# Down stage of an encoder layer: seven products on shared PSUM banks, with kept operands and a reordered end

## The chip, the cores and the metric

The kernel runs on one core of a Trainium2 chip. The metric is the device time of one execution in microseconds (us), lower is better; a kernel's time is the median of its runs.

## The reference, cut to what matters

One encoder layer (a token mixer, then a gated feed-forward block with a convolution of width 3) runs on 256 + 1024 = 1280 tokens of 1024 channels, all in fp32. The change lies in the last matrix product and in what follows it:

```python
D_FF = ((8 * D_MODEL // 3 + 127) // 128) * 128        # 2816
def conv_ffn(h, w_up, w_conv, b_conv, w_down):
    ...
    gate, val = jnp.split(up, 2, axis=-1)
    return (jax.nn.silu(gate) * val) @ w_down
...
        y = conv_ffn(h, w_up[l], w_conv[l], b_conv[l], w_down[l])
        x = x + gate2 * rmsnorm(y, g_post_ffn[l])
```

So y = G · W, G of 1280 x 2816 and W (`w_down`) of 2816 x 1024, then a root-mean-square norm of each row of y, a gain per column and an addition to x.

## The kernel before, in words

**Products.** TensorE takes every fp32 matrix product as three products of operands that are each split into a high and a low part (`split`, L89: ScalarE rounds the high part to fp32r, VectorE subtracts it from the source to get the low part). `mmk` (L1150) issues the three 128 x 128 by 128 x 512 matmuls high·high, high·low and low·high into one PSUM bank.

**Strassen.** The Down stage halves each of the three dimensions and uses Strassen's seven products M1 to M7 in place of eight block products. G is kept transposed in DRAM (`g_d`, one tensor per 128 of the 2816 inner rows), and its blocks are A00, A01, A10, A11 (first index: the half of the tokens, 640 each; second: even or odd 128-row slice of the inner dimension). B00 to B11 are the blocks of W (first index: the same even or odd slice; second: the half of the 1024 output columns). Each product has 11 steps k over 128 inner rows and 5 tiles j of 128 tokens, so 11 · 5 · 3 = 165 matmuls. The table `prods` (L1311) gives the order M3, M5, M1, M7, M4, M2, M6, the operands of each (a block, or a sum or difference of two blocks) and where its result goes: output block (half of the tokens, half of the columns) and how (`set`, `neg`, `add`, or subtract).

**Steps.** `ops_of(i, k)` (L1322) loads the blocks of a step with DMAs on SyncE's queue, makes the sum or difference on VectorE (`saM` of 640 columns for A, `sbM` of 512 for B, L1330) and splits both into `aoM` and `boM`. Rings limit how far this runs ahead: 4 tiles for A loads, 4 raw tiles for B loads (`raw_d`), 2 for each sum, 4 for `aoM`, 5 for `boM`. The diagonal blocks A00 and A11 stay on chip from their first load (`ares`, L1273), and so does B11 for the first 7 steps (`bres`, L1274). All other blocks are loaded again for each product that uses them.

**Banks.** Each product takes 5 of the 8 PSUM banks in rotation (`bank`, L1145), one per tile j; 3 of them were not used by the product before. After two starting steps, which are run together for the tiles 0, 1, 2 and then for 3, 4, TensorE goes step by step over all five tiles. The last 2 steps (the last 4 of M6) are run tile by tile, and after each tile `evac` (L1372) brings the bank to the output rows `y` in SBUF: ScalarE copies (`set`, `neg`), VectorE adds or subtracts.

**End of a block.** When the last product that goes into an output block is in, `finish` (L1339) takes the sum of squares on ScalarE (`junk`) and multiplies by the gain on VectorE (`yg`, L1345). When both column halves of a tile are finished, `emit` (L1351) makes the row factor `rf` on GpSimd (L1359, L1360). For the tiles of the first half of the tokens, ScalarE scales the rows and GpSimd starts an adding DMA to the output, spread over the steps of the next product (`later`). For the second half, whose tiles end in M6, x was put into the output earlier and is loaded again into `xo` (three buffers, L1365); VectorE multiplies by `rf` and adds (L1368, two halves of 512 columns), and SyncE's queue stores each half (L1370).

**Order.** TensorE's order is the program's. The instructions of ScalarE, VectorE, GpSimd and SyncE's queue are put in order within each engine by a planner from its own estimate of times and the order of the program as priority; on the chip each queue then runs strictly in that order, so an instruction that waits holds up what stands behind it.

Of the kernel before, what the change touches and what calls it, by code (L numbers as in the profile page):

```python
# [8 lines left out]
F32 = mybir.dt.float32  # L9
# [3 lines left out]
AF = mybir.ActivationFunctionType  # L13
ALU = mybir.AluOpType
# [20 lines left out]
def encoder_kernel(ctx: ExitStack, tc: tile.TileContext, x_prompt, x_sample, c_prompt, c_sample,  # L35
# [3 lines left out]
    nc = tc.nc  # L39
# [13 lines left out]
    def out_rows(t):  # L53
        return out_p[0, P * t:P * t + P, :] if t < 2 else out_s[0, P * (t - 2):P * (t - 1), :]
# [34 lines left out]
    def split(w, raw, eng=None):  # L89
        nc.scalar.activation(w[:, 0, :], raw, AF.Copy)  # L90
        (eng or nc.gpsimd).tensor_tensor(out=w[:, 1, :], in0=raw, in1=w[:, 0, :].bitcast(F32), op=ALU.subtract)  # L91
# [327 lines left out]
    for ev in CFG["ord"].split():  # L419
# [6 lines left out]
        else:  # L426
            f = affine_h1 if ev[0] in "AB" else low_h1
# [388 lines left out]
    for g in range(4 * NT):  # L816
        gi, t = g // NT, g % NT
# [71 lines left out]
    with tc.high_priority():  # L889
# [14 lines left out]
                                   op0=ALU.add, op1=ALU.mult)  # L904
# [175 lines left out]
    for f in range(F0):  # L1080
        ps = fp.tile([P, 2, 256], F32, tag="f", name=f"upP_{f}")
        ws = []
        for half in range(2):
            for kh in range(2):
                with tc.issue_after(mloads[6].ins if f == 0 else xloads[NT - 1].ins) if f < 2 else ExitStack():
                    raw = load_up(f, half, kh, f"raw_p{f}_{half}{kh}")
                w = fslot(f"wp{f}_{half}{kh}")
# [57 lines left out]
    def bank(name):  # L1145
        i = banks["i"] % 8
        banks["i"] += 1
        return gpa.tile([P, 512], F32, tag="g", name=name) if i in (3, 4) else fp.tile([P, 512], F32, tag="f", name=name)

    def mmk(ps, ao, w, j, k):  # L1150
        cs_ = slice(P * j, P * j + P)
        for q, (ai, wi) in enumerate(((0, 0), (0, 1), (1, 0))):
            nc.tensor.matmul(ps, ao[ai][:, cs_], w[wi], start=(k == 0 and q == 0), stop=(k == NK - 1 and q == 2))  # L1153
# [129 lines left out]
    for k in range(NK - 1, NE - 1, -1):  # L1283
        new_ar(0, k)
        if k < 7:
            new_br(k)
    loaded = set()

    def load_a(r, c, k):
        if r == c:  # L1290
            if (r, k) not in loaded:
                loaded.add((r, k))
                nc.sync.dma_start(ares[(r, k)], g_d[2 * k + c][r])
            return ares[(r, k)]
        t = new_as(f"A{r}{c}_{k}")
        nc.sync.dma_start(t, g_d[2 * k + c][r])
        return t

    def load_b(c, n, k):
        if c and n and ("b", k) in loaded:  # L1300
            return bres[k]
        f = 2 * k + c
        if c and n and k < 7:
            raw = bres[k]
            loaded.add(("b", k))
        else:
            raw = raw_tile(f"raw_d{c}{n}_{k}")
        nc.sync.dma_start(raw, w_down[P * f:P * f + P, 512 * n:512 * n + 512])
# [9 lines left out]
    y, ygs = {}, {}  # L1318
    ssq = {t: dn.tile([P, 2], F32, name=f"fssq{t}") for t in range(NT)}
    done = set()  # L1320

    def ops_of(i, k):  # L1322
        name, a, b, _ = prods[i]
        src = []
        for what, terms, load, n, tag in ((0, a, load_a, 640, "sa"), (1, b, load_b, 512, "sb")):
            t0 = load(*terms[0], k)
            if len(terms) > 1:
                t1 = load(*terms[1], k)
                s = new_sum(tag, n, f"{tag}{name}_{k}")
                nc.vector.tensor_tensor(out=s, in0=t0, in1=t1, op=ALU.add if terms[2] > 0 else ALU.subtract)  # L1330
                t0 = s
            src.append(t0)
        ao = new_ao(f"ao{name}_{k}")
        split(ao, src[0], nc.vector)
        wo_ = new_bo(f"bo{name}_{k}")
        split(wo_, src[1], nc.vector)
        return [[t[:, h, :] for h in range(2)] for t in (ao, wo_)]

    def finish(t, n):  # L1339
        junk = dn.tile([P, 512], BF16, tag="junk", name=f"junk{t}_{n}", bufs=1)  # L1340
        cs_ = slice(512 * n, 512 * n + 512)
        nc.scalar.activation(junk, y[t][:, cs_], AF.Square, scale=1.0 / 32, accum_out=ssq[t][:, n:n + 1])  # L1342
        yg = y[t][:, cs_] if (t, 1 - n) not in done else dn.tile([P, 512], F32, tag="yg" if t in half_tiles[1] else "yh", name=f"yg{t}", bufs=2 if t in half_tiles[1] else 5)
        ygs[(t, n)] = yg
        nc.vector.tensor_tensor(out=yg, in0=y[t][:, cs_], in1=Gbc2[:, 0 if t < 2 else 1, cs_], op=ALU.mult)  # L1345
# [3 lines left out]
    later = []  # L1349

    def emit(t, n):  # L1351
        def scaled():
            for n in range(2):
                cs_ = slice(512 * n, 512 * n + 512)
                nc.scalar.activation(y[t][:, cs_], ygs[(t, n)], AF.Copy, scale=r)
                nc.gpsimd.dma_start(out_rows(t)[:, cs_], y[t][:, cs_], accum_op=ALU.add)

        r = dn.tile([P, 1], F32, tag="rf", name=f"rf{t}", bufs=6)
        nc.gpsimd.tensor_tensor(out=r, in0=ssq[t][:, 0:1], in1=ssq[t][:, 1:2], op=ALU.add)  # L1359
        nc.gpsimd.tensor_tensor(out=r, in0=r, in1=mhalf, op=ALU.pow)  # L1360
# [4 lines left out]
        nc.sync.dma_start(xo, out_rows(t))  # L1365
        for n in range(2):
            cs_ = slice(512 * n, 512 * n + 512)
            nc.vector.scalar_tensor_tensor(out=xo[:, cs_], in0=ygs[(t, n)], scalar=r, in1=xo[:, cs_],  # L1368
                                           op0=ALU.mult, op1=ALU.add)
            nc.sync.dma_start(out_rows(t)[:, cs_], xo[:, cs_])  # L1370

    def evac(i, j, ps):  # L1372
        for r, n, how in prods[i][3]:
            t = half_tiles[r][j]
            if t not in y:
                y[t] = dn.tile([P, D], F32, name=f"y{t}")
            d = y[t][:, 512 * n:512 * n + 512]
            if how == "set":
                nc.scalar.activation(d, ps, AF.Copy)
            elif how == "neg":  # L1380
                nc.scalar.activation(d, ps, AF.Copy, scale=-1.0)
            elif how == "add":
                nc.vector.tensor_tensor(out=d, in0=ps, in1=d, op=ALU.add)  # L1383
            else:
                nc.vector.tensor_tensor(out=d, in0=d, in1=ps, op=ALU.subtract)  # L1385
        for r, n, how in prods[i][3]:
            t = half_tiles[r][j]
            if not any((r, n) == q[:2] for p in prods[i + 1:] for q in p[3]):
                finish(t, n)
                done.add((t, n))  # L1390
                if (t, 1 - n) in done:
                    emit(t, n)

    for i in range(len(prods)):
        last = i == len(prods) - 1
        pss = [bank(f"dn{i}_{j}") for j in range(5)] if i else pss0
        ops = {}
        tail = 4 if last else 2
        for k in range(0 if i else NE, NK - tail):
            ops[k] = ops_of(i, k)  # L1400
            if i and k == 0:
                continue
            if i and k == 1:
                for js in ((0, 1, 2), (3, 4)):
                    for kk in range(2):
                        for j in js:
                            mmk(pss[j], *ops[kk], j, kk)
                continue
            for j in range(5):
# [40 lines left out]
```

## Time and profile before

| | |
|---|---|
| median of 3 runs | 1454.65 us (1453.76 to 1455.06) |
| profiled execution, its own time | 1453.5 us |
| profiled execution, span | 1451.8 us |
| busy share of TensorE, VectorE, ScalarE, GpSimd | 95%, 71%, 47%, 38% |
| Down stage's first and last matmul | 1160.5 us, 1440.8 us |
| mean granted clock of TensorE | 0.980 of full speed |

A line of the grouped view gives the source line, engine, operation, output and inputs with their shapes, the count, then total busy time and the mean of one in ns, then the engine's idle time just before these instructions and what ended it. In a timeline a row gives the start, the duration, the engine, the instructions merged into it with their count, and in brackets the idle time before and its releaser. A row of the windows gives, for a stretch of time, each engine's busy time and instruction count, the granted clock, the share of the 16 DMA engines and the rate in GB/s. TensorE's instructions overlap, so its pace is read from counts, not from their durations.

### The profile page before, as it was taken

Reading aid. Unit: us, or ns where it says so; the run is one execution under the profiler, and the core shown is the slowest. Engines: PE = TensorE matmul, PEld = TensorE weight load, DVE = VectorE, ACT = ScalarE, POOL = GpSimd, SP = SyncE. Lnnn points to the kernel's source line nnn. Section 1 sums busy time; section 2 is a strip of 40 time slices with the busy share of each in tenths; the row PEclk is TensorE's granted clock in tenths of the full one; section 3 lists DMA queues with packets and bytes.
Section 4 is the critical chain, followed back from the end, with each engine's and each line's share of the span. In section 5 each row is a group of like instructions: output and inputs, shape, how many; then the busy total and the mean of one; then the engine's idle time right before and its main releaser. Section 6 shows DMA issues by size and latency. Waiting matters only on the chain. (4 is left out here: it accounts for less than half of the span.)

```text
span 1451.8 us, 20330 instructions
## 1 busy us (share of the span) xinstructions
PE 1377.5 (95%) x7057; PEld 1132.6 (78%) x7057; DVE 1031.5 (71%) x1619; ACT 677.9 (47%) x1379; POOL 546.8 (38%) x664
## 2 busy tenths in 40 slices
PE   8999989898999999888999999999999989999996
PEld 6786667676788788877888888887888768888875
DVE  5675667878845456896657566678788576996777
ACT  3543465644433333565444454544555345533632
POOL 3346755787764111434333333344444100000301
PEclk9999999999999999999999999999999999999998
DMA  9657542332233632552221212122222478365764
GB/s 287 218 211 268 184 151 74 111 111 69 83 105 113 215 112 83 168 150 83 80 63 61 82 59 84 56 92 67 84 87 87 147 245 299 106 197 178 161 206 163
DMA packets 178011, 195.91 MB, mean 135 GB/s; under 512 B 12152, under 2 KB 132020, under 8 KB 175604
## 3 DMA queue, kind: packets, MB, share of 16 engines
q1 hardware_dynamic: 170760, 176.83, 37.9%
q10 hardware_dynamic: 5468, 14.38, 2.9%
q0 software_dynamic: 1680, 3.41, 1.3%
q8 instruction: 55, 0.90, 0.3%
q14 instruction: 48, 0.39, 0.1%
HBM read 156.55 MB, written 38.03 MB: 134 GB/s over the span
## 5 line engine op out<-in xcount | busy, mean ns | idle before, releaser
L1153 PE MATMUL dn<-boM,aoM 128*128 128x512 f32 x1140 | 268.2, 398 | 8.9 <-ACT boM L90 5.1
L1153 PEld LDWEIGHTS dn<-boM,aoM 128*128 128x128 f32 x1140 | 218.5, 192 | 58.6 <-ACT boM L90 6.4
L91 POOL TENSOR_TENSOR ws<-raw_s,ws 128x512 fp32r<-128x512 f32 x56 | 88.5, 1584 | 166.0 <-ACT ws L90 165.0
L91 POOL TENSOR_TENSOR ws_S<-S,ws_S 128x512 fp32r<-128x512 f32 x66 | 102.0, 1547 | 128.2 <-ACT ws_S L90 128.1
L1210 PE MATMUL upX<-bop_T,ws_S 128*128 128x512 f32 x528 | 130.5, 397 | 6.2 <-ACT ws_S L90 3.3
L1210 PEld LDWEIGHTS upX<-bop_T,ws_S 128*128 128x128 f32 x528 | 100.0, 191 | 27.7 <-ACT ws_S L90 3.5
L338 PE MATMUL ps_ga<-w_a,h1hi 128*128 128x512 f32 x320 | 104.6, 404 | 5.4 <-POOL w_a L91 4.4
L338 PE MATMUL ps_gb<-w_b,h1hi 128*128 128x512 f32 x320 | 105.0, 409 | 1.6 <-DVE w_b L91 1.1
L90 ACT ACTIVATE ws_S<-S 128x512 fp32r<-128x512 f32 x88 | 54.8, 629 | 76.7 <-PE upX L1210 27.6
L1043 DVE SCALAR_TENSOR_TENSOR ag<-ug,c,ag 128x1023 f32<-128x1023 f32 x44 | 67.7, 1540 | 24.1 <-ACT ag L1047 23.3
L338 PEld LDWEIGHTS ps_ga<-w_a,h1hi 128*128 128x128 f32 x320 | 59.3, 191 | 25.1 <-issue 6.7
L1201 PEld LDWEIGHTS upQ<-hp,ws 128*128 128x128 f32 x576 | 72.3, 191 | 1.9
L90 ACT ACTIVATE ws<-raw_s 128x512 fp32r<-128x512 f32 x78 | 48.6, 626 | 52.6 <-issue 26.2
L1201 PE MATMUL upQ<-hp,ws 128*128 128x256 f32 x576 | 72.8, 283 | 0.0
L1097 PE MATMUL upP<-hp,wp 128*128 128x256 f32 x480 | 62.1, 290 | 11.2 <-DVE wp L91 8.3
L1097 PEld LDWEIGHTS upP<-hp,wp 128*128 128x128 f32 x480 | 59.7, 196 | 13.3 <-DVE wp L91 9.5
L1178 DVE TENSOR_TENSOR S<-raw_s,raw_s 128x512 f32<-128x512 f32 x44 | 53.7, 1221 | 22.1 <-DMA raw_s<-in_w_up_dram 18.2
L90 ACT ACTIVATE aoM<-saM 128x640 fp32r<-128x640 f32 x55 | 40.4, 738 | 62.1 <-issue 24.5
L338 PEld LDWEIGHTS ps_gb<-w_b,h1hi 128*128 128x128 f32 x320 | 57.8, 191 | 14.6 <-issue 2.6
L97 POOL TENSOR_TENSOR rstd<-ms,mhalf 128x2 f32<-128x2 f32 (+1 forms) x90 | 65.7, 730 | 7.3
L880 PE MATMUL y<-wo,mh 128*128 128x512 f32 x160 | 64.0, 400 | 2.1 <-ACT mh L794 2.1
L1210 PE MATMUL upV<-bop,ws_S 128*128 128x512 f32 x264 | 63.6, 390 | 1.9 <-ACT uv L1225 1.9
(289 smaller groups left out, 3227.8 us busy)
## 6 DMA issues: line engine op xcount, KB each, us to landing
raw_d<-in_w_down_dram SPq DMA_DIRECT2D x103, 256.0 KB
raw_s<-in_w_up_dram SPq DMA_DIRECT2D x88, 256.0 KB
A<-g_d SPq DMA_DIRECT2D x66, 320.0 KB
wa<-in_w_ada_dram SPq DMA_DIRECT2D x16, 1024.0 KB
g_d<-av SPq DMA_DIRECT2D x21, 512.0 KB
raw_p<-in_w_up_dram SPq DMA_DIRECT2D x40, 256.0 KB
wa<-in_w_ada_dram SPq DMA_DIRECT2D x16, 512.0 KB
vr_d<-vr SPq DMA_DIRECT2D x20, 256.0 KB
```

The source lines that it names most:

```text
L90: nc.scalar.activation(w[:, 0, :], raw, AF.Copy)
L91: (eng or nc.gpsimd).tensor_tensor(out=w[:, 1, :], in0=raw, in1=w[:, 0, :].bitcast(F32), op=ALU.subtract)
L97: nc.gpsimd.tensor_tensor(out=r, in0=ms, in1=mhalf.to_broadcast([P, n]) if n > 1 else mhalf, op=ALU.pow)
L338: nc.tensor.matmul(ps, st, mv, start=(i == 0), stop=(i == n - 1))
L880: nc.tensor.matmul(ys[n], mh[:, kt, :], wos[(kt, n)][:, 0, :], start=(i == 0), stop=False)
L1043: nc.vector.scalar_tensor_tensor(out=acc[:, o:o + b - a], in0=src[:, a:b], scalar=c2[:, i, fi:fi + 1], in1=acc[:, o:o + b - a], op0=ALU.mu ...
L1097: nc.tensor.matmul(ps[:, half, :], st, hp[:, hi, kt, :], start=(kt == 0 and i == 0 and half == 0), stop=(kt == KT - 1 and i == 2), skip_gr ...
L1153: nc.tensor.matmul(ps, ao[ai][:, cs_], w[wi], start=(k == 0 and q == 0), stop=(k == NK - 1 and q == 2))
L1178: nc.vector.tensor_tensor(out=s, in0=a, in1=b, op=op)
L1201: nc.tensor.matmul(Q[:, half, :], st, hp[:, hi, kt, :], start=(kt == 0 and i == 0 and half == 0), stop=(kt == KT - 1 and i == 2), skip_gro ...
L1210: nc.tensor.matmul(ps, w[:, wi, P * j:P * j + P], bops[(b, j)][:, hi, :], start=(start and j == 0 and i == 0), stop=(stop and j == 3 and i ...
```

## The change

It touches the Down stage alone.

1. **Shared banks.** M5 and M2 are computed with the sign turned (their B operand is negated in the split: ScalarE copies with scale -1, VectorE uses a scalar_tensor_tensor in place of a tensor_tensor). M1 then accumulates on M5's banks, M7 on M1's, and M6 on M2's, so that these banks hold M1 - M5, M1 - M5 + M7 and M6 - M2. Only M3, M5, M4 and M2 take new banks. A bank is read by `evac` at the end of M5, M1 and M2 and then written further. VectorE's evacuations fall from 40 to 25, ScalarE's from 20 to 15. Block (0, 1) is finished after M1, not after M5, since M1's evacuation (`over`) reads it.
2. **Kept operands.** From M4 on B00 of the first 7 steps goes into the tiles of B11, whose last use is M7, and M2 and M6 read it there. In M2, A10 of steps 5 to 10 is loaded into the tiles of A11 of steps 0 to 5, and M6 reads it there.
3. **Differences made early.** M6's operand A10 - A00 is made during M2 for steps 0 to 4, in A00's tile.
4. **End.** The two multiply-and-add instructions of an `xo` tile and its stores are held back until the gain multiplication (`yg`) of the next tile has been placed, and the second half's store goes to ScalarE's queue.

```diff
-    def mmk(ps, ao, w, j, k):
+    def mmk(ps, ao, w, j, k, first=True):
...
-            nc.tensor.matmul(ps, ao[ai][:, cs_], w[wi], start=(k == 0 and q == 0), stop=(k == NK - 1 and q == 2))
+            nc.tensor.matmul(ps, ao[ai][:, cs_], w[wi], start=(first and k == 0 and q == 0),
+                             stop=(k == NK - 1 and q == 2), skip_group_check=True)
...
-        t = new_as(f"A{r}{c}_{k}")
+        if r and k >= NPC:
+            t = ares[(1, k - NPC)]
+            if ("a10", k) in loaded:
+                return t
+            loaded.add(("a10", k))
+        else:
+            t = new_as(f"A{r}{c}_{k}")
...
-        if c and n and k < 7:
+        if late_b and not c and not n and k < 7:
+            if ("b00", k) in loaded:
+                return bres[k]
+            loaded.add(("b00", k))
+            raw = bres[k]
+        elif c and n and k < 7:
...
-    prods = (("M3", ((0, 0),), ((0, 1), (1, 1), -1), ((0, 1, "set"), (1, 1, "set"))),
-             ("M5", ((0, 0), (0, 1), 1), ((1, 1),), ((0, 1, "add"), (0, 0, "neg"))),
-             ("M1", ((0, 0), (1, 1), 1), ((0, 0), (1, 1), 1), ((0, 0, "add"), (1, 1, "add"))),
-             ("M7", ((0, 1), (1, 1), -1), ((1, 0), (1, 1), 1), ((0, 0, "add"),)),
+    prods = (("M3", ((0, 0),), ((0, 1), (1, 1), -1), ((0, 1, "set"),)),
+             ("M5", ((0, 0), (0, 1), 1), ((1, 1),), ((0, 1, "sub"),)),
+             ("M1", ((0, 0), (1, 1), 1), ((0, 0), (1, 1), 1), ((1, 1, "over"), (0, 1, None))),
+             ("M7", ((0, 1), (1, 1), -1), ((1, 0), (1, 1), 1), ((0, 0, "set"),)),
              ("M4", ((1, 1),), ((1, 0), (0, 0), -1), ((0, 0, "add"), (1, 0, "set"))),
-             ("M2", ((1, 0), (1, 1), 1), ((0, 0),), ((1, 0, "add"), (1, 1, "sub"))),
+             ("M2", ((1, 0), (1, 1), 1), ((0, 0),), ((1, 0, "sub"),)),
              ("M6", ((1, 0), (0, 0), -1), ((0, 0), (0, 1), 1), ((1, 1, "add"),)))
+    negated, chained = ("M5", "M2"), ("M1", "M7", "M6")
...
+    NPC = 5
...
+            if name == "M6" and what == 0 and k < NPC:
+                src.append(ares[(0, k)])
+                continue
...
+        if name == "M2" and k < NPC:
+            nc.vector.tensor_tensor(out=ares[(0, k)], in0=t_a10, in1=ares[(0, k)], op=ALU.subtract)
         wo_ = new_bo(f"bo{name}_{k}")
-        split(wo_, src[1], nc.vector)
+        if name in negated:
+            nc.scalar.activation(wo_[:, 0, :], src[1], AF.Copy, scale=-1.0)
+            nc.vector.scalar_tensor_tensor(out=wo_[:, 1, :], in0=src[1], scalar=-1.0, in1=wo_[:, 0, :].bitcast(F32),
+                                           op0=ALU.mult, op1=ALU.subtract)
+        else:
+            split(wo_, src[1], nc.vector)
...
-        for n in range(2):
-            cs_ = slice(512 * n, 512 * n + 512)
-            nc.vector.scalar_tensor_tensor(out=xo[:, cs_], in0=ygs[(t, n)], scalar=r, in1=xo[:, cs_],
-                                           op0=ALU.mult, op1=ALU.add)
-            nc.sync.dma_start(out_rows(t)[:, cs_], xo[:, cs_])
+
+        def added():
+            for n in range(2):
+                cs_ = slice(512 * n, 512 * n + 512)
+                nc.vector.scalar_tensor_tensor(out=xo[:, cs_], in0=ygs[(t, n)], scalar=r, in1=xo[:, cs_],
+                                               op0=ALU.mult, op1=ALU.add)
+                (nc.scalar if n else nc.sync).dma_start(out_rows(t)[:, cs_], xo[:, cs_])
+
+        late_adds.append(added)
...
-            elif how == "neg":
-                nc.scalar.activation(d, ps, AF.Copy, scale=-1.0)
+            elif how == "over":
+                nc.vector.tensor_tensor(out=d, in0=ps, in1=y[half_tiles[0][j]][:, 512 * n:512 * n + 512], op=ALU.add)
...
-        pss = [bank(f"dn{i}_{j}") for j in range(5)] if i else pss0
+        first = prods[i][0] not in chained
+        if first:
+            pss = [bank(f"dn{i}_{j}") for j in range(5)] if i else pss0
         ops = {}
+        if prods[i][0] == "M4":
+            late_b.append(True)
...
             evac(i, j, pss[j])
+            if len(late_adds) > 1:
+                with tc.issue_after(last_yg[0].ins):
+                    late_adds.pop(0)()
+    while late_adds:
+        late_adds.pop(0)()
```

More of the change, by code (lines that the diff above doesn't have):

```diff
@@ L1286, in encoder_kernel @@
             new_br(k)
-    loaded = set()
+    loaded, late_b = set(), []
     def load_a(r, c, k):
@@ L1309, in load_b @@
         return raw
-    prods = (("M3", ((0, 0),), ((0, 1), (1, 1), -1), ((0, 1, "set"), (1, 1, "set"))),
-             ("M5", ((0, 0), (0, 1), 1), ((1, 1),), ((0, 1, "add"), (0, 0, "neg"))),
-             ("M1", ((0, 0), (1, 1), 1), ((0, 0), (1, 1), 1), ((0, 0, "add"), (1, 1, "add"))),
-             ("M7", ((0, 1), (1, 1), -1), ((1, 0), (1, 1), 1), ((0, 0, "add"),)),
+    prods = (("M3", ((0, 0),), ((0, 1), (1, 1), -1), ((0, 1, "set"),)),
[3 rows of a table added]
              ("M4", ((1, 1),), ((1, 0), (0, 0), -1), ((0, 0, "add"), (1, 0, "set"))),
-             ("M2", ((1, 0), (1, 1), 1), ((0, 0),), ((1, 0, "add"), (1, 1, "sub"))),
+             ("M2", ((1, 0), (1, 1), 1), ((0, 0),), ((1, 0, "sub"),)),
              ("M6", ((1, 0), (0, 0), -1), ((0, 0), (0, 1), 1), ((1, 1, "add"),)))
+    negated, chained = ("M5", "M2"), ("M1", "M7", "M6")
     y, ygs = {}, {}
+    last_yg = [None]
     ssq = {t: dn.tile([P, 2], F32, name=f"fssq{t}") for t in range(NT)}
     done = set()
+    NPC = 5
     def ops_of(i, k):
@@ L1325, in ops_of @@
         for what, terms, load, n, tag in ((0, a, load_a, 640, "sa"), (1, b, load_b, 512, "sb")):
+            if name == "M6" and what == 0 and k < NPC:
+                src.append(ares[(0, k)])
+                continue
             t0 = load(*terms[0], k)
+            if name == "M2" and what == 0:
+                t_a10 = t0
             if len(terms) > 1:
@@ L1344, in finish @@
         ygs[(t, n)] = yg
-        nc.vector.tensor_tensor(out=yg, in0=y[t][:, cs_], in1=Gbc2[:, 0 if t < 2 else 1, cs_], op=ALU.mult)
+        last_yg[0] = nc.vector.tensor_tensor(out=yg, in0=y[t][:, cs_], in1=Gbc2[:, 0 if t < 2 else 1, cs_], op=ALU.mult)
         if (t, 1 - n) not in done:
             nc.gpsimd.tensor_scalar(ssq[t][:, n:n + 1], ssq[t][:, n:n + 1], EPS, None, op0=ALU.add)
-    later = []
+    later, late_adds = [], []
     def emit(t, n):
@@ L1379, in evac @@
                 nc.scalar.activation(d, ps, AF.Copy)
-            elif how == "neg":
-                nc.scalar.activation(d, ps, AF.Copy, scale=-1.0)
+            elif how == "over":
+                nc.vector.tensor_tensor(out=d, in0=ps, in1=y[half_tiles[0][j]][:, 512 * n:512 * n + 512], op=ALU.add)
             elif how == "add":
                 nc.vector.tensor_tensor(out=d, in0=ps, in1=d, op=ALU.add)
-            else:
+            elif how == "sub":
                 nc.vector.tensor_tensor(out=d, in0=d, in1=ps, op=ALU.subtract)
@@ L1406, in encoder_kernel @@
                         for j in js:
-                            mmk(pss[j], *ops[kk], j, kk)
+                            mmk(pss[j], *ops[kk], j, kk, first)
                 continue
             for j in range(5):
-                mmk(pss[j], *ops[k], j, k)
+                mmk(pss[j], *ops[k], j, k, first)
             if later and k > 1:
@@ L1416, in encoder_kernel @@
             for k in range(NK - tail, NK):
-                mmk(pss[j], *ops[k], j, k)
+                mmk(pss[j], *ops[k], j, k, first)
             evac(i, j, pss[j])
+            if len(late_adds) > 1:
[3 more added lines that the diff above has]
+        late_adds.pop(0)()
     for close in (fp_close, gpa_close, dn_close, dr_close, rp_close, cp_close, dram_close):
```

## The prediction

> **What bounds the kernel now.** The page first, then TensorE's timeline in the Down stage.
>
> ```profile
> span 1451.8 us, 20330 instructions
> PE 14%; DVE 4%; DMA 1%; ACT 1%; issue 1%; POOL 0%; DVEq 0%; POOLq 0%; ACTq 0%; SPq 0%
> L1153 PE MATMUL dn<-boM,aoM 128*128 128x512 f32 x1140 | 268.2, 398 | 8.9 <-ACT boM L90 5.1
> ```
> ```profile
> 1160.46 3.56 PE L1153 MATMUL dn<-ebo,eao 128*128 128x512 f32 x15
> 1168.56 218.16 PE L1153 MATMUL dn<-boM,aoM 128*128 128x512 f32 x947 [4.54 <-ACT boM L90]
> 1387.09 1.10 PE L1153 MATMUL dn<-boM,aoM 128*128 128x512 f32 x3 [0.37 <-DVE aoM L91]
> 1390.82 34.65 PE L1153 MATMUL dn<-boM,aoM 128*128 128x512 f32 x137 [2.62 <-DVE aoM L91]
> 1426.27 0.73 PE L1153 MATMUL dn<-boM,aoM 128*128 128x512 f32 x2 [0.81 <-DVE boM L91]
> 1427.53 13.65 PE L1153 MATMUL dn<-boM,aoM 128*128 128x512 f32 x51 [0.53 <-ACT boM L90]
> ```
>
> TensorE leads the chain and works through M3 to M4 without a gap. It waits at three places: at the start, after 947 - 150 - 4·165 = 137 matmuls of M2 (its steps 9 and 10), and before M6's last four steps. The last matmul ends at 1427.53 + 13.65 = 1441.18, so 10.6 us of the span follow it. Matmul counts in windows price the gaps:
>
> ```profile
> 1164.00:1176.00 12.00, 7.46 (x20) 0.72 0.62 215
> 1176.00:1384.00 208.00, 208.00 (x919) 1.00 0.65 202
> 1386.00:1398.00 12.00, 9.01 (x26) 0.72 0.79 260
> 1424.00:1434.00 10.00, 8.62 (x29) 0.83 0.05 18
> ```
>
> The pace without gaps is 208/919 = 0.2263 us per matmul. The M2 window should hold 12/0.2263 = 53.0 and holds 26: 27.0 · 0.2263 = 6.1 us lost. The M6 window should hold 44.2 and holds 29: 3.4 us lost. Both are more than the waits shown (2.99 and 1.34 us), because the clock is halved afterwards:
>
> ```profile
> 1390.00:1392.00 2.00, 1.18 (x3) 0.51 0.71 226
> 1428.00:1430.00 2.00, 2.00 (x5) 0.50 0.00 0
> ```
>
> [...]
>
> **M2's stall.** VectorE's and SyncE's timelines there, and a window with the busy time and count of PE, PEld, DVE, ACT and POOL, the clock, the DMA share and GB/s:
>
> ```profile
> 1377.67 0.83 DVE L1330 TENSOR_TENSOR saM<-A,A 128x640 f32<-128x640 f32 x1 [0.88 <-DMA A<-g_d]
> 1385.61 0.69 DVE L1330 TENSOR_TENSOR sbM<-raw_d,raw_d 128x512 f32<-128x512 f32 x1 [7.11 <-DMA raw_d<-in_w_down_dram]
> 1389.34 0.69 DVE L1330 TENSOR_TENSOR sbM<-raw_d,raw_d 128x512 f32<-128x512 f32 x1 [0.97 <-DMA raw_d<-in_w_down_dram]
> 1389.94 0.82 DVE L91 TENSOR_TENSOR aoM<-saM,aoM 128x640 fp32r<-128x640 f32 x1
> ```
> ```profile
> 1376.82 0.33 SPq L1308 DMA_DIRECT2D raw_d<-in_w_down_dram  x1
> 1386.33 1.66 SPq L1308 DMA_DIRECT2D raw_d<-in_w_down_dram  x3
> ```
> ```profile
> 1366.00:1386.00 20.00, 20.00 (x90) 16.58 (x89) 11.01 (x16) 9.64 (x16) 4.16 (x5) 1.00 1.07 284
> ```
>
> M2 has no sum in B, so the two `sbM` are M6's first steps, planned ahead of M2's last low parts (the `aoM` behind them). They wait for raw loads, and M2's operands wait behind them. A load issued at 1376.82 lands near 1385.6, since the DMA engines are full (share 1.07); the next three could issue only at 1386.33, when raw tiles came free.
>
> The change attacks this twice. Volume: M2 and M6 each skip 7 loads of B00, and M6 skips 11 of A10.
>
> ```profile
> raw_d<-in_w_down_dram SPq DMA_DIRECT2D x99, 256.0 KB
> A<-g_d SPq DMA_DIRECT2D x61, 320.0 KB
> ```
>
> That is 14 · 256 + 11 · 320 = 7.1 MB; 7 of them, 1.8 MB, leave M2, or 6.3 us at the 284 GB/s of the row. Ring: M2's raw tiles are then used only by its steps 7 to 10, and M6's steps 0 to 3 need one raw tile each instead of two. M6's steps 0 and 1 wait for M2's steps 7 and 8 instead of 7 to 10, so the second `sbM` gets its tile two steps (2 · 15 · 0.2263 = 6.8 us) earlier; its late start cost 2.62 of the 2.99 us. Either alone about covers the delay. I take the stall as gone: -6.1 us, with 0 as the other bound.
>
> New waits there: A10 of step k >= 5 waits on SyncE's queue for M2's sum of step k - 5, with later A and B loads queued behind it. Four A tiles and these sums lie a whole ring ahead of TensorE, so I cost it at nothing; without that cover a load is late and costs another such stall. The new A10 - A00 must wait in VectorE's order until M2's sum and split have read A10; it frees the A tile that the load of step 4 needs. Priced below.
>
> **M6's stall.** VectorE is behind, busy for 23.22 of 23.80 us before it:
>
> ```profile
> 1404.40:1428.20 23.80, 23.22 (x35) 0.99 0.52 166
> ```
> ```profile
> 1405.02 0.81 DVE L91 TENSOR_TENSOR aoM<-saM,aoM 128x640 fp32r<-128x640 f32 x1
> 1405.75 0.68 DVE L91 TENSOR_TENSOR boM<-sbM,boM 128x512 fp32r<-128x512 f32 x1
> 1406.36 0.81 DVE L1330 TENSOR_TENSOR saM<-A,A 128x640 f32<-128x640 f32 x1
> 1407.09 0.68 DVE L91 TENSOR_TENSOR boM<-sbM,boM 128x512 fp32r<-128x512 f32 x1
> ```
>
> From start to start a 640 instruction costs 0.73 us and a 512 one 0.61 (a scalar_tensor_tensor 0.67, by the `xo` rows below). A step of M6 needs two of each, 2.68 us, so 11 steps take 29.5; M2's evacuation stands in front with 10 adds and 5 gain products, 15 · 0.61 = 9.1. Sum 38.6 us, against 165 · 0.2263 = 37.3 for TensorE. After: 5 steps without the A sum, 25.8, plus 5 + 5 instructions, 6.1: 31.9 us. VectorE then has 5.4 us in hand: -3.4 us. The 5 · 0.73 = 3.7 us move into M2, whose VectorE sum then is 11 steps of 2 · 0.73 + 0.67, the five differences, and M4's evacuation of 10 · 0.61: 23.4 + 3.7 + 6.1 = 33.2 of 37.3 us. The cover is thinner (4 us), and if it went, M2 would lag as M6 does now.
>
> Evacuations and negation elsewhere:
>
> ```profile
> L1385 DVE TENSOR_TENSOR y<-y,dn 128x512 f32<-128x512 f32 x5 | 3.4, 676 | 0.0
> L1368 DVE SCALAR_TENSOR_TENSOR xo<-y,rf,xo 128x512 f32<-128x512 f32 x5 | 3.8, 751 | 5.1 <-POOL rf L1360 5.1
> L1379 ACT ACTIVATE y<-dn 128x512 f32<-128x512 f32 x15 | 8.4, 594 | 1.8 <-DVE y L1383 1.0 <-PE dn L1153 0.8
> ```
>
> 15 fewer VectorE evacuations save 9 us of that engine, 5 copies 3 us of ScalarE; 22 negated splits cost 22 · (0.751 - 0.676) = 1.7 us more. All lies beside TensorE's gapless M5 to M4: nothing on the path.
>
> **The end.** VectorE is late there:
>
> ```profile
> 1440.85 0.68 DVE L1383 TENSOR_TENSOR y<-dn,y 128x512 f32<-128x512 f32 x1
> 1444.62 0.68 DVE L1383 TENSOR_TENSOR y<-dn,y 128x512 f32<-128x512 f32 x1
> 1447.05 0.75 DVE L1368 SCALAR_TENSOR_TENSOR xo<-y,rf,xo 128x512 f32<-128x512 f32 x1 [1.02 <-POOL rf L1360]
> 1447.72 0.75 DVE L1368 SCALAR_TENSOR_TENSOR xo<-yg,rf,xo 128x512 f32<-128x512 f32 x1
> ```
>
> A tile costs 3.77 us, 1.02 of it waiting for `rf`; TensorE delivers one per 12 · 0.2263 = 2.72. The last add starts at 1444.62, 3.44 us after the last matmul. With the previous tile's two instructions in the wait's place, a tile takes 2 · 0.61 + 2 · 0.67 = 2.56 us, under 2.72, so the last add follows the last matmul: -3.4 us. The last tile's own latency (1447.05 - 1444.62 = 2.43) stays. Next late is its `xo` load, which reuses the buffer of the second tile, stored later than now:
>
> ```profile
> 1441.40 0.40 SPq L1365 DMA_DIRECT2D xo<-out_dram  x1
> ```
> ```profile
> 1442.50:1444.60 2.10, 0.00 (x0) 1.00 0.77 254
> 1448.50:1450.10 1.60, 0.00 (x0) 0.50 0.88 328
> ```
>
> That load lands 3.2 us after its issue (DMA activity ends near 1444.6), a store 1.6 us after its add ends (1448.47 to 1450.1). With T the end of the first tile's matmuls, the second tile's adds follow the third tile's add and gain product and end at T + 2 · 2.72 + 1.22 + 0.67 + 0.75 = T + 8.1, the load lands at T + 12.9 and is needed at T + 4 · 2.72 + 2.43 = T + 13.3. If the fourth tile's load, on its way then, slows it by 1 us, it is 0.6 us late. I take 0.3: the end gives -3.1 us, between 0 and -3.4. The store moved to ScalarE's queue saves nothing, since its add ends last; a square behind it comes a tile later.
>
> **Sum.** -6.1 - 3.4 - 3.1 = -12.6 us: 1453.5 to 1440.9 for the profiled execution. The median shown, 1454.65, lies 1.15 us above it; the forecast against that median is 1442.0. The start's stall stays: nothing ahead of it is touched.
>
> **Rivals.**
>
> *A. One piece is not earned, or one new stall appears.* Any of: M2 stalls still, because a sum for M6 waits in VectorE's strict order ahead of M2's operands (1442.0 + 6.1 = 1448.1); M6 stalls (1445.4); the last `xo` load is placed behind the fourth tile's store, issued at T + 10.9 + 1.2 + 0.7 and landing at T + 16.0, 2.7 us late (1444.4), or the adds do not move on VectorE at all, so that the change does not do what it says (1445.1). For: the old stall too came from the planner's order, which no row of before shows for the new program. Against: each has a margin above.
>
> *B. Slower: the shared banks.* Now three of the five banks of a new product are free from the start; on a shared bank the first matmul of M1, M7 and M6 must wait until VectorE has read it.
>
> ```profile
> 1275.93 4.88 DVE L1383 TENSOR_TENSOR y<-dn,y 128x512 f32<-128x512 f32 x8
> ```
>
> This is M1's evacuation: it ran promptly while TensorE went on. A bank is reused 4 · 6 · 0.2263 = 5.4 us after its last matmul, and evacuating all five takes 5 · 0.61 = 3.1 us, or 6.1 with M1's and M2's gain products between. So VectorE may lag by several instructions, but not stand 7.11 us before a DMA as it did in M2. If it does at all three seams, each costs about what M2's stall did: 3 · 6.1 = 18.3, and 1442.0 + 18.3 = 1460.3. Slower begins where a seam costs over 12.6/3 = 4.2 us. [...] No run here shows two products on one bank in this stage.
>
> *C. No change.* The saved transfers were hidden, the planner makes another order with one full stall and one seam wait of the same size, 12.2 us: 1454.2. For: M3 to M4 are gapless with full rings, so a seam has much to lose. Against: the loads beside the stall share full DMA engines, and VectorE's work in M6 falls below TensorE's.
>
> **How the numbers follow.** The forecast as it stands 0.62; A 0.22; B 0.07; C 0.09. About 0.2% (2.9 us) is what a measurement can tell from no change. Faster needs under 1451.7: forecast and A, 0.84. Same, to 1457.6: C less its slow edge, 0.08. Slower: B and that edge, 0.08. The range runs from 1439.6 (the lowest run, 1453.76, less the full 6.1 + 3.4 + 3.4, less the runs' spread of 1.3) to 1449.0 (A's dearest case, 1448.1, and 0.9 of spread): it leaves out B and C, 0.16.
>
> **What would show it.** TensorE's timeline: one row of matmuls from about 1168.6 to near 1431.7 (1441.18 - 9.5), without a gap at M2's steps 9 and 10 or before M6's tail, and no clock row of 0.5 after the start. DMA share in M2 under 1.0. `xo` rows that wait for neither GpSimd nor, by more than 0.6 us, a DMA, and a last add within 0.1 us of the last matmul. I am wrong if matmuls at the start of M1, M7 or M6 wait for VectorE's `y` (B), if VectorE still waits for `raw_d` in M2 or M6 (A), or if the last `xo` add stands more than 3 us after the last `y` add.

## The result, and the profile after

The changed kernel takes 1443.13 us (median of 4 runs, 1439.27 to 1445.26) against 1454.2 us before (median of 4, 1452.56 to 1455.06): ratio 0.9931, 95% interval 0.9914 to 0.9948. The forecast was 1442.0 us. The time fell by 11.1 us where 12.6 were forecast, but of the forecast's three terms only the two in the matmuls came; the third, the end, did not. The profiled execution took 1445.21 us. From the page of the kernel after:

```profile
span 1443.5 us, 20263 instructions
PE 16%; DVE 2%; DMA 1%; ACT 1%; issue 0%; POOL 0%; DVEq 0%; POOLq 0%; ACTq 0%
L1153 PE MATMUL dn<-boM,aoM 128*128 128x512 f32 x1140 | 261.6, 392 | 4.9 <-ACT boM L90 4.5
```

TensorE's idle time in this group fell from 8.9 to 4.9 us, and 4.5 of these are the start's wait. VectorE's share of the chain fell from 4% to 2%. TensorE's timeline in the Down stage of the kernel after:

```profile
1162.46 3.56 PE L1153 MATMUL dn<-ebo,eao 128*128 128x512 f32 x15
1170.57 225.22 PE L1153 MATMUL dn<-boM,aoM 128*128 128x512 f32 x981 [4.54 <-ACT boM L90]
1396.10 36.36 PE L1153 MATMUL dn<-boM,aoM 128*128 128x512 f32 x159 [0.31 <-DVE y L1417]
```

Six rows became three. The 981 matmuls run from M3 through M2 into M6's start without a gap, so both old stalls are gone. The one wait left, 0.31 us, is new: M6's matmul waits until VectorE has read M2's bank (`y`, L1417), which M6 now goes on writing. The last matmul ends at 1396.10 + 36.36 = 1432.46.

The stage starts at a different time in each execution (1158.3 to 1163.1 us over all traces here), through work ahead of it that no kernel here touches. So the stage is compared from its first matmul: 1432.46 - 1162.46 = 270.0 us of matmuls, against 1441.18 - 1160.46 = 280.7 before. After the last matmul, 11.0 us of span follow, against 10.6 before. That is 281.0 us against 291.3 for the stage. The whole gain is in the matmuls, and the end gave nothing.

VectorE's timeline in M2, kernel after:

```profile
1374.93 0.82 DVE L1351 TENSOR_TENSOR saM<-A,A 128x640 f32<-128x640 f32 x1
1380.92 0.69 DVE L1351 TENSOR_TENSOR sbM<-B,raw_d 128x512 f32<-128x512 f32 x1 [5.17 <-DMA raw_d<-in_w_down_dram]
1383.60 0.68 DVE L1351 TENSOR_TENSOR sbM<-B,raw_d 128x512 f32<-128x512 f32 x1
```

M6's first sum still stands ahead of M2's last low parts and still waits for its load, 5.17 us instead of 7.11. The second sum, which waited 0.97 us and started 3.73 us after the first, now starts 2.68 us after it, without a wait. A window with all engines, the clock, the DMA share and GB/s, kernel after:

```profile
1368.00:1388.00 20.00, 20.00 (x90) 16.57 (x89) 14.80 (x23) 10.84 (x19) 3.54 (x5) 1.00 0.83 193
```

The DMA engines are no longer full there (0.83 against 1.07), and VectorE gets more done (14.80 us busy against 11.01). The end of the kernel after, rows of its whole timeline:

```profile
1429.61 0.37 SPq L1393 DMA_DIRECT2D xo<-out_dram  x1
1429.82 0.34 ACTq L1400 DMA_DIRECT2D out_dram<-xo  x1
1431.88 0.33 SPq L1400 DMA_DIRECT2D out_dram<-xo  x1
1432.49 0.69 DVE L1415 TENSOR_TENSOR y<-dn,y 128x512 f32<-128x512 f32 x1
1434.08 0.55 POOL L1387 TENSOR_TENSOR rf<-fssq 128x1 f32<-128x1 f32 x1 [1.15 <-ACT junk L1370]
1434.39 0.34 SPq L1393 DMA_DIRECT2D xo<-out_dram  x1
1438.69 0.75 DVE L1398 SCALAR_TENSOR_TENSOR xo<-y,rf,xo 128x512 f32<-128x512 f32 x1 [3.46 <-DMA xo<-out_dram]
```

The last `y` add starts 0.03 us after the last matmul, where it was 3.44 us late before. Then VectorE stands 3.46 us for the last `xo` load, which could be issued only at 1434.39. SyncE's waits in this part, with the total, the number of times and the longest:

```profile
SPq L1393 <- DMA out_dram<-xo: 2.1, 1, 2.1
```

The load stands on SyncE's queue behind the third tile's store (issued at 1431.88, after its add), and then waits 2.1 us more for the second tile's store, whose buffer it takes. That store was issued at 1429.82 on ScalarE's queue and the wait for it ended near 1434.3, 4.5 us later; the fourth tile's load, issued at 1429.61, ran beside it.

### The profile page after: what moved, and what is told of

The parts are those of the page before. It is cut to its first block, busy times and chain, and to the rows that moved or that the text cites. A ratio compares the mean times of both kernels' runs of the same rounds, so it can differ in the third digit from the quotient of the medians.

```text
span 1443.5 us, 20263 instructions
## 1 busy us (share of the span) xinstructions
PE 1370.0 (95%) x7057; PEld 1130.9 (78%) x7057; DVE 1025.5 (71%) x1604; ACT 674.9 (47%) x1374; POOL 548.6 (38%) x664
## 3 DMA queue, kind: packets, MB, share of 16 engines
q0 software_dynamic: 1680, 3.41, 1.3%
## 5 line engine op out<-in xcount | busy, mean ns | idle before, releaser
L1153 PE MATMUL dn<-boM,aoM 128*128 128x512 f32 x1140 | 261.6, 392 | 4.9 <-ACT boM L90 4.5
L1153 PEld LDWEIGHTS dn<-boM,aoM 128*128 128x128 f32 x1140 | 215.2, 189 | 51.3 <-ACT boM L90 5.0
L90 ACT ACTIVATE aoM<-saM 128x640 fp32r<-128x640 f32 x50 | 36.8, 739 | 74.4 <-PE dn L1153 34.7
```

What stands on the lines that cost most here:

```text
L1153: nc.tensor.matmul(ps, ao[ai][:, cs_], w[wi], start=(first and k == 0 and q == 0), stop=(k == NK - 1 and q == 2), skip_group_check=True)
```

## The experiments

All kernels are compared by the stage in their traces, since its length repeats for the changed kernel within 0.2 us, while its runs spread over 6 us (1439.27 to 1445.37). "Matmuls" runs from the stage's first matmul to the end of its last one, "end" from there to the end of the span.

| kernel | time, us | matmuls | end | stage |
|---|---|---|---|---|
| before, first trace | 1453.5 | 280.7 | 10.6 | 291.3 |
| before, second trace (before_again) | 1454.18 | 278.0 | 11.4 | 289.5 |
| after, first trace | 1445.21 | 270.0 | 11.0 | 281.0 |
| after, second trace (after_again) | 1441.93 | 270.1 | 11.1 | 281.2 |
| xo4 | 1438.04 | 269.8 | 8.0 | 277.8 |
| old_end | 1445.26 | 269.8 | 11.6 | 281.4 |
| ring_only | 1451.25 | 277.6 | 10.4 | 288.0 |
| banks_only | 1450.08 | 275.4 | 11.5 | 286.8 |
| banks_again | 1448.71 | 275.6 | 11.5 | 287.0 |
| no_banks | 1442.94 | 270.2 | 11.1 | 281.3 |
| no_kept | 1447.32 | 275.3 | 10.6 | 285.9 |
| no_early | 1441.19 | 270.4 | 10.8 | 281.2 |
| kept_only | 1445.19 | 272.4 | 11.4 | 283.8 |
| adds_in_m6 | 1452.71 | 277.6 | 11.4 | 289.0 |

The times are those of the profiled executions; where no median is given below, there was one run. The stage of the order of before varies more than that of the change: 289.0 to 291.3 us over its three traces (before, before_again and adds_in_m6, whose edit moved nothing).

**The changed kernel once more (after_again).** No edit.

> The changed kernel itself, timed beside the others. Its first four runs spread from 1439.3 to 1445.3 us. If the spread comes from stretches ahead of the Down stage, the Down stage alone (first dn matmul to the end of the span) is again 281.0 us, 10.3 us under the kernel before, while the start of the stage moves by some us from profile to profile; if it comes from the Down stage, that figure moves by several us instead. Time about 1443 us, ratio 0.993.

Median 1443.33 us (6 runs, 1441.93 to 1445.37), ratio 0.9942 (0.9930 to 0.9954) against 1451.98 us for the kernel before on the same chip. The stage repeats (281.2 us), the wait for the last load too. So the late load belongs to the program and not to one execution. Against this chip's median the change is worth 8.65 us.

**A fourth `xo` buffer (xo4).** The kernel after, with one buffer more:

```diff
-        xo = dn.tile([P, D], F32, tag="xo", name=f"xo{t}", bufs=3)
+        xo = dn.tile([P, D], F32, tag="xo", name=f"xo{t}", bufs=4)
```

> Four xo buffers instead of three: the fourth tile's load goes out long before the end and the fifth's takes the buffer of the first tile, stored some 5 us before. Theory 1 (the last xo load is late because its buffer comes free late and shares the DMA engines with stores): the wait of 3.46 us before the last multiply-and-add goes, the end after the last matmul falls from 11.0 to about 7.6 us, time about 3.4 us under the changed kernel (near 1439.7 us, ratio 0.991). Rival (the end is set by rf and the store): the wait moves to GpSimd's rf and the time stays within 0.5 us of the changed kernel.

Median 1439.41 us (4 runs, 1438.04 to 1440.28), ratio 0.9913 (0.9900 to 0.9926): the best kernel here. Rows of its whole timeline at the end:

```profile
1425.44 0.37 SPq L1393 DMA_DIRECT2D xo<-out_dram  x1
1428.33 0.69 DVE L1415 TENSOR_TENSOR y<-dn,y 128x512 f32<-128x512 f32 x1
1429.66 0.74 DVE L1398 SCALAR_TENSOR_TENSOR xo<-y,rf,xo 128x512 f32<-128x512 f32 x1
1429.91 0.55 POOL L1387 TENSOR_TENSOR rf<-fssq 128x1 f32<-128x1 f32 x1 [1.15 <-ACT junk L1370]
1430.54 0.94 POOL L1388 TENSOR_TENSOR rf<-rf,mhalf 128x1 f32<-128x1 f32 x1
1431.51 0.75 DVE L1398 SCALAR_TENSOR_TENSOR xo<-y,rf,xo 128x512 f32<-128x512 f32 x1 [0.44 <-POOL rf L1388]
```

The last load now takes the first tile's buffer and is issued 2.9 us before the last `y` add instead of 1.9 us after it. The wait of 3.46 us is gone, and the end takes 8.0 us instead of 11.1. That shows the buffer to be what cost the end its gain. What is left is 0.44 us for `rf`.

**The old end (old_end).** The kernel after, with the adds and both stores put back where the kernel before has them:

```diff
-        def added():
-            for n in range(2):
-                ...
-                (nc.scalar if n else nc.sync).dma_start(out_rows(t)[:, cs_], xo[:, cs_])
-        late_adds.append(added)
+        for n in range(2):
+            ...
+            nc.sync.dma_start(out_rows(t)[:, cs_], xo[:, cs_])
```

> The changed kernel with the old end: adds directly behind each tile's own, both stores on SyncE's queue. Theory 1 (what the held-back adds earned is lost again to the xo load): the end after the last matmul is 10.6 us as in the kernel before, against 11.0 with the new end, so the time is within 0.5 us of the changed kernel. Rival (the new end earned the 3.1 us that the prediction gave it): 3.1 us slower, near 1446.2 us.

Median 1445.49 us (6 runs, 1442.02 to 1446.48), ratio 0.9950 (0.9937 to 0.9963), an interval that overlaps the changed kernel's. Two rows of VectorE's timeline at its end:

```profile
1436.32 0.68 DVE L1411 TENSOR_TENSOR y<-dn,y 128x512 f32<-128x512 f32 x1
1438.76 0.75 DVE L1396 SCALAR_TENSOR_TENSOR xo<-y,rf,xo 128x512 f32<-128x512 f32 x1 [1.02 <-POOL rf L1388]
```

The last add starts 4.3 us after the last matmul (1432.05), even later than the 3.44 us of before, and the wait of 1.02 us for `rf` is back; but the load is in time. Its end is only 0.5 us longer than that of the change: the change traded one wait for another.

**The ring alone (ring_only).** The kernel before, with M2's first seven B00 loads put into B11's tiles. All loads are still made, so the bytes are those of before; only the ring of raw tiles is relieved.

```diff
-        if c and n and k < 7:
+        if m2 and not c and not n and k < 7:
+            raw = bres[k]
+        elif c and n and k < 7:
```

> The kernel before with one edit: B00 of steps 0 to 6 is loaded for M2 into the tiles of B11 instead of raw tiles; every transfer is still made. Theory 1 (M2's stall comes from the ring of raw tiles and VectorE's strict order): M2 runs without a gap although the bytes are the same, 6.1 us faster, near 1448 us, ratio 0.996; M6 still stalls. Rival (the DMA engines are full, the bytes decide): sums of M6 still wait several us for raw_d ahead of M2's last low parts, the gap of 2 to 3 us and the half clock stay, time 1454 us.

Median 1450.69 us (10 runs, 1444.49 to 1454.76), ratio 0.9985 (0.9968 to 1.0001). VectorE's timeline in M2, then TensorE's:

```profile
1383.08 0.69 DVE L1332 TENSOR_TENSOR sbM<-raw_d,raw_d 128x512 f32<-128x512 f32 x1 [6.63 <-DMA raw_d<-in_w_down_dram]
1386.42 0.69 DVE L1332 TENSOR_TENSOR sbM<-raw_d,raw_d 128x512 f32<-128x512 f32 x1 [0.57 <-DMA raw_d<-in_w_down_dram]
```
```profile
1387.90 12.99 PE L1153 MATMUL dn<-boM,aoM 128*128 128x512 f32 x56 [0.69 <-DVE aoM L91]
1403.58 18.43 PE L1153 MATMUL dn<-boM,aoM 128*128 128x512 f32 x80 [2.69 <-DVE boM L91]
```

M2's gap falls from 2.62 us (0.43 + 2.19 in the second trace of before) to 0.69: the ring alone cures most of it. But where 6.1 us were expected, little or nothing is won: the matmuls take 277.6 us, as in adds_in_m6 with its full gap in M2. VectorE still stands 6.63 us for its load, and M6 then stalls 2.69 us behind it and 0.61 + 0.81 + 0.53 + 0.23 before its tail, 4.87 us in all where the second trace of before has 3.33.

**The banks alone (banks_only, banks_again).** The kernel before with part 1 of the change, run twice:

```diff
+    negated, chained = ("M5", "M2"), ("M1", "M7", "M6")
...
+        first = prods[i][0] not in chained
+        if first:
+            pss = [bank(f"dn{i}_{j}") for j in range(5)] if i else pss0
```

> The kernel before with the shared banks alone (negated M5 and M2, chained M1, M7, M6); no kept operands, no early differences, old end. Judged by the Down stage from its first matmul to the end of the span: 291.3 us before, 281.0 and 281.2 in two profiles of the change. Theory 1 (each stall has its own cause): M2's stall stays, since its loads are as before; M6's VectorE sum falls by five adds to 35.6 us, under TensorE's 37.3, so M6's stall goes: -3.4 us, 287.9. Rival (sharing banks makes waits of its own at the seams): matmuls of M1, M7 or M6 wait some us for y adds and the stage stays at 291 or more.

> The kernel before with the shared banks alone, once more. In its first profile M2's gap of 2.23 us was followed by full clock. If the gap's length decides, again full clock and a stage of 286.8 us; if its place in time decides, half clock for some us in this profile or not, with the same gap: a stage of 286.8 to 290 us.

Stage 286.8 and 287.0 us. TensorE's timeline of the first run:

```profile
1390.86 6.97 PE L1153 MATMUL dn<-boM,aoM 128*128 128x512 f32 x28 [2.23 <-DVE aoM L91]
1398.00 0.96 PE L1153 MATMUL dn<-boM,aoM 128*128 128x512 f32 x3 [0.18 <-DVE y L1392]
1400.54 36.40 PE L1153 MATMUL dn<-boM,aoM 128*128 128x512 f32 x159 [1.57 <-DVE y L1392]
```

M2's gap stays. M6's stall is gone, since VectorE has fewer evacuations, and a wait of 0.18 + 1.57 us on the shared banks at the seam from M2 to M6 (where the one ends and the other begins) stands in its place. The seams of M1 and M7 show no wait. The second run repeats this: 0.36 + 2.32 us in M2, 0.18 + 1.58 at the seam.

**The change without the banks (no_banks).** The kernel after, with the old table of products and

```diff
-    negated, chained = ("M5", "M2"), ("M1", "M7", "M6")
+    negated, chained = (), ()
```

> The changed kernel without the shared banks: the seven products as before on banks of their own, 40 VectorE evacuations, no negation; kept operands, early differences and new end stay. Theory 1: M2 runs without a gap, and M6's VectorE sum is 25.8 + 9.1 = 34.9 us, still under 37.3, so M6 does not stall: the Down stage is within 0.5 us of the change's 281.1. Rival (the evacuations that the banks save are what M6 needed): M6 stalls again, 284.5 us.

Stage 281.3 us, as with the banks. TensorE's timeline has one gap, in M6:

```profile
1399.37 30.71 PE L1153 MATMUL dn<-boM,aoM 128*128 128x512 f32 x134 [0.86 <-DVE boM L91]
```

**The change without the early differences (no_early).** Both conditions that make and use them are set to False:

```diff
-            if name == "M6" and what == 0 and k < NPC:
+            if False:
...
-        if name == "M2" and k < NPC:
+        if False:
```

> The changed kernel without the early differences: M6 loads A10 of steps 0 to 4 and makes all eleven A differences itself; the rest stays. Theory 1 (M6's stall is VectorE's sum against TensorE's): 29.5 + 6.1 = 35.6 us, 1.7 us in hand, so no stall or a small one: Down stage 281 to 282 us. Rival (the differences are what removed M6's stall): 3.4 us more, 284.5 us.

Stage 281.2 us, again no loss; the matmuls alone take 270.4 us, 0.3 to 0.4 more than the change. TensorE's one gap is the wait for the shared banks at the seam from M2 to M6, longer than with the differences:

```profile
1392.39 36.35 PE L1153 MATMUL dn<-boM,aoM 128*128 128x512 f32 x159 [1.16 <-DVE y L1417]
```

**The change without the kept operands (no_kept).** All B00 and A10 are loaded again, as before:

```diff
-        if r and k >= NPC:
+        if False:
...
-        if late_b and not c and not n and k < 7:
+        if False:
```

> The changed kernel without the kept operands: B00 and A10 (steps 5 to 10) are loaded again for M2 and M6 through the rings; banks, early differences and new end stay. Theory 1 (M2's stall came from the loads): it returns, +6.1 us on the Down stage, 287.2. Rival (a lighter VectorE is enough): no gap in M2, 281.1 us.

Stage 285.9 us: 4.7 to 4.9 are lost, where 6.1 were expected. Two rows of TensorE's timeline, then a window of 12 us around the gap (PE busy with its count, the clock, the DMA share, GB/s):

```profile
1389.65 8.70 PE L1153 MATMUL dn<-boM,aoM 128*128 128x512 f32 x31 [2.23 <-DVE aoM L91]
1398.60 36.34 PE L1153 MATMUL dn<-boM,aoM 128*128 128x512 f32 x159 [0.26 <-DVE y L1417]
```
```profile
1385.00:1397.00 12.00, 9.55 (x34) 0.86 0.83 276
```

M2's stall is back as it was. The window should hold 53 matmuls and holds 34: 19 · 0.2263 = 4.3 us. The wait at the seam to M6, on the second row, stays small (0.26 us).

**The kept operands alone (kept_only).** The kernel before with part 2 of the change (both hunks of loads, and `late_b` set at M4):

```diff
+        if r and k >= NPC:
+            t = ares[(1, k - NPC)]
...
+        if late_b and not c and not n and k < 7:
...
+            raw = bres[k]
```

> The kernel before with the kept operands alone (B00 of 7 steps from M4 on, A10 of steps 5 to 10 from M2 on); banks, differences and end as before. Theory 1 (two stalls with two causes): M2's gap goes, but M6's VectorE sum stays at 38.6 us against TensorE's 37.3 and M6 still stalls: Down stage 291.3 - 6.1 = 285.2 us. Rival (M6's stall only followed from M2's): both go, 291.3 - 9.5 - 0.8 = 281 us.

Stage 283.8 us, 5.7 less than the second trace of before. TensorE's timeline:

```profile
1167.77 230.11 PE L1153 MATMUL dn<-boM,aoM 128*128 128x512 f32 x1006 [4.54 <-ACT boM L90]
1399.43 18.66 PE L1153 MATMUL dn<-boM,aoM 128*128 128x512 f32 x81 [1.56 <-DVE boM L91]
```

M2 has no gap. M6 still waits for VectorE's low parts: 1.56 us here, and 0.36 + 0.53 + 0.23 later.

**The kernel before once more (before_again).** No edit.

> The kernel before once more, for its trace. The queue orders are fixed, so the gaps of M2 (0.37 and 2.62 us) and M6 (0.81 and 0.53 us) come again within some tenths. If the half clock behind a gap follows from the gap's length, the stage is again 291.3 us; if it follows from where the gap falls against a clock of its own, the stage is up to 6 us shorter with the same gaps.

TensorE's timeline, then windows of 12 us around its two gaps (columns as above):

```profile
1392.00 12.96 PE L1153 MATMUL dn<-boM,aoM 128*128 128x512 f32 x56 [2.19 <-DVE aoM L91]
1407.68 20.63 PE L1153 MATMUL dn<-boM,aoM 128*128 128x512 f32 x83 [2.71 <-DVE boM L91]
```
```profile
1386.00:1398.00 12.00, 9.38 (x40) 1.00 0.82 275
1402.00:1414.00 12.00, 9.29 (x35) 0.86 0.30 89
```

The same program stalls by about as much in M2, but at full clock (1.00): 13 · 0.2263 = 2.9 us are lost instead of 6.1. M6's stall comes earlier in the product and is longer (2.71 us, and 0.39 + 0.23 later, instead of 1.34 in all); after it the clock is halved (0.50 from 1408 to 1410), and in its window 18 · 0.2263 = 4.1 us are lost.

**The adding DMAs moved (adds_in_m6).** Meant to take bytes out of M2 without touching the ring, by placing GpSimd's adding DMAs later in the program:

```diff
-            if later and k > 1:
+            if later and k > 1 and last:
```

> The kernel before with the ten adding DMAs of the first half of the tokens, and the scaling before them, moved from M2's steps to M6's; the rings and the loads stay. [...] Theory 1 (raw tiles come free late whatever the load): VectorE still waits some us for raw_d and M2 has a gap of 1 us or more.

In the trace they are still issued at 1354.7 to 1372 us, inside M2 as before: the later place in the program did not move them in time. So this run tells nothing of bytes; it is in effect a third trace of the order of before, with gaps of 0.44 + 2.19 us in M2, 2.75 + 0.20 + 0.22 in M6, and a stage of 289.0 us.

## Why the prediction was right, and where it failed

**M2's stall: right in mechanism and cure.** The gap is gone. The kept operands are what does it: it is absent in kept_only and back in no_kept. The ring alone, with all the bytes, takes it from about 2.6 to 0.69 us, so "either alone about covers the delay" holds for the ring up to that rest; for the bytes alone it stays open, as adds_in_m6 did not move them. One sign was badly chosen: VectorE "still waits for `raw_d`" in M2, 5.17 us, and TensorE has no gap, because the load behind it now comes in time.

**M6's stall: right in cure, but not a term of its own.** VectorE's sum of 38.6 us stands against TensorE's 37.3, and left as it was (kept_only), the stall stays. The shared banks leave out five adds (38.6 - 5 · 0.61 = 35.6), the early differences five sums (38.6 - 5 · 0.73 = 34.9). With the differences alone (no_banks) M6 still waits 0.86 us for an operand; with the banks alone (no_early) the one gap left, 1.16 us, is the wait for the shared banks at the seam; both (31.9) leave 0.31 of that. In the stage's length the second of them no longer shows: 281.3 and 281.2 us with one, 281.0 and 281.2 with both. M2's thinner cover held.

But the sum alone does not set the stall: it fits the 1.34 us of the first trace, in which TensorE itself lost 6.1 us in M2, and not the 3.33 of the second. In ring_only M2's gap shrinks by 1.93 us and M6's waits grow by 1.54, with nothing won, while VectorE's waits for `raw_d` in M2 stay (6.63 + 0.57 us); kept_only, where that wait is 5.33 us in all, wins 5.2 us or more in the stage. The waits read as one lag of VectorE behind both stalls, where the prediction priced them as two terms; it took both, so its sum is not hurt.

**The size of the two: 10.7 us measured, 9.5 (6.1 + 3.4) forecast, and both hang on the trace taken as before.** Against the three traces of the order of before (280.7, 278.0 and 277.6 us of matmuls) the gain is 7.6 to 10.7 us. The difference lies in the clock: 0.51 after M2's gap in the first trace, 1.00 in the others. The prediction counted a halved clock as part of each stall, as if it came each time. The waits alone of the first trace, 2.99 + 1.34 = 4.3 us, lie well below the gain against each of the three. In the first pair 0.9 us of the 10.7 is the start's clock too, since its window of 12 us holds 24 matmuls after and held 20 before (4 · 0.2263 = 0.9).

**The end: the step that failed.** It was to give -3.1 us, and gave +0.4 against the first trace of before and -0.3 to -0.4 against the other two traces of that order. The first half of the step held: adds come every 2.72 us, VectorE waits for `rf` nowhere, the last `y` add follows the last matmul. The failing term is the last load's: "the load lands at T + 12.9", which stood on a store landing 1.6 us after its add (a price from the idle end of the kernel before) and a load of 3.2 us. With T = 1421.58, the second tile's adds end at T + 8.2 as worked out, but its store takes 4.5 us beside the fourth load, the last load is issued at T + 12.8 and takes 4.3 us itself. It lands at T + 17.1 against a need at T + 13.3. xo4, where that load has a buffer early, gets 11.1 - 8.0 = 3.1 us back. The prediction's own sign fired: the last `xo` add starts 6.2 us after the last `y` add, where more than 3 was to mean that it is wrong. Rival A had this item, with another cause (the fourth tile's store) and 2.7 us; it is the third and second tile's stores, and 3.46 us. That the store takes long because of the load beside it is not shown apart. The end of xo4 is still 0.5 us longer than the forecast's 10.6 - 3.1 = 7.5: from the last `y` add to its `xo` add it takes 1431.51 - 1428.33 = 3.18 us, where the prediction kept 2.43, because `rf` comes later.

**That the time came so near is in part luck.** In the first pair of traces the stage gained 10.3 us: 10.7 in the matmuls, 0.9 of them from the start's clock, and nothing at the end. The second pair gained 8.3 (289.5 to 281.2) and the medians on the second chip differ by 8.65, both some 4 us short of 12.6. The 11.1 us between the first medians also hold differences ahead of the stage, whose start varies by up to 4.8 us between traces.

**Evacuations and negation elsewhere: nothing, as costed.** The 1.7 us that the negated splits were to cost VectorE are not there either. From the grouped view of the kernel after:

```profile
L1361 DVE SCALAR_TENSOR_TENSOR boM<-B,boM 128x512 fp32r<-128x512 f32 x14 | 9.6, 683 | 0.0
L91 DVE TENSOR_TENSOR boM<-sbM,boM 128x512 fp32r<-128x512 f32 x54 | 36.9, 685 | 2.9 <-ACT boM L90 2.7
L1398 DVE SCALAR_TENSOR_TENSOR xo<-y,rf,xo 128x512 f32<-128x512 f32 x5 | 3.7, 745 | 3.5 <-DMA xo<-out_dram 3.5
```

The negating scalar_tensor_tensor takes 683 ns, a tensor_tensor 685. Only the `xo` form, from which the prediction took its price, takes 745; its scalar is a column `rf`, the other's a constant.

**Rival B is there in small.** At M6's seam TensorE waits for `y`: 0.31 us in the change, 1.75 us with the banks alone. The seams of M1 and M7 have no wait. The kept operands are not what keeps it small: with them and without the early differences (no_early) it is 1.16 us, with the differences and without them (no_kept) 0.26. In banks_only, where the seam costs 1.75 us, a sum of M6 for A stands on VectorE between M2's `y` adds (`saM` at 1398.47, between `y` at 1397.27 and at 1399.81). The differences take such sums away: between the `y` adds of the change, from 1391.74 to 1397.50, there is none. In no_kept TensorE also comes to the seam later, by its own stall (0.21 + 2.23 us).

**Rival C** fell: the time changed, and kept_only alone shortens the stage by 5.2 to 7.5 us against the three traces of the order of before. Whether fewer bytes or the freed ring did this, kept_only does not separate.

## What to carry to other kernels

An instruction of a later stage that is planned ahead of the current one's operands turns a late load into a stall of the current stage (here 7.11 us on VectorE, 0.37 + 2.62 on TensorE); look for it where an engine waits for data that no one needs yet, and try giving the load its buffer earlier. Here that cut the gap from 2.62 to 0.69 us with the same bytes, but brought no time until the engine that lagged had less to do as well: stalls that one engine's lag causes are priced together, not one by one. When work is held back to keep an engine in step, follow the buffers that it holds: price the store that frees them and the load that refills them beside each other (4.5 and 4.3 us here), and not by rows from an idle end (1.6 and 3.2). Take a second trace of the kernel before when a stall's price includes a clock that drops, since M2's gap (2.62 and 2.99 us) cost 2.9 us in one execution and 6.1 in another.

## What the runs showed of the hardware

**The clock after a gap is not set by the gap's length alone.** With gaps of 2.69 us (ring_only) and 2.23 us (banks_only) the clock stayed at 1.00; after 2.23 us in no_kept and 2.71 in before_again it was halved for 3.4 us (0.86 over 12 us), and after M2's 2.62 in the first trace of before for 6.8 (0.72 over 12 us). Two windows of 12 us, of ring_only and of banks_only, around these gaps:

```profile
1399.00:1411.00 12.00, 9.31 (x42) 1.00 0.37 104
```
```profile
1385.00:1397.00 12.00, 9.54 (x40) 1.00 0.87 285
```

Windows of 0.1 us show more. In the first trace of before the clock is 0.50 from 1168.16 to 1174.99, from 1390.03 to 1396.86 and from 1427.58 to 1430.99: 6.83, 6.83 and 3.41 us, the first two twice the third. These stretches begin 221.87 and 37.55 us apart, 65 and 11 steps of 3.413 us. In the kernel after there is one, behind the stage's start (1168.30 to 1175.13, 6.83 us), and no other up to the last matmul. Windows of 2 us show one of 3.4 us in each of no_kept, before_again, adds_in_m6 and ring_only, from 1389.20, 1407.56, 1406.08 and 1426.08.

From these starts follows an estimate: steps of 3.413 us, counted back from the stretch, cut ring_only's gap of 2.69 us into 1.3 and 1.4, while 2.6 of before_again's 2.71 us lie within one step. So a gap's place against the steps fits the difference; that the steps go on between the stretches is not shown. How much idle time within a step it takes stays open: by the same count M2's gap in adds_in_m6 has 1.7 us in one and the clock stays at 1.00, while 0.81 and 0.53 us before M6's tail in the first trace of before were followed by 0.50. The longest gap after the stage's start in these traces is 2.75 us (adds_in_m6, M6), with 0.52 behind it.

**GpSimd's small operations took longer while VectorE added.** The two that make `rf` take 0.19 and 0.55 us in old_end and in the kernel before, where VectorE waits for them (1.02 us), and 0.55 and 0.94 in the kernel after and in xo4 from the second tile on, where it runs the previous tile's `xo` adds. That is 0.75 us, all that the last `xo` add of xo4 comes later after its `y` add. No run separated VectorE's adds from other causes.
